# ConvFFN: a fifth buffer for the raw weights, and the partial sums p5 in the place of the constants

## The chip, the core and the metric

The kernel runs on one core of a Trainium2 chip. The metric is the device time of one launch in microseconds, as the median of several runs. A profiled execution has, beside its time, a span: from its first to its last instruction.

## What is computed

One block of a streaming encoder over 512 frames of 1024 channels: two recurrent branches that are merged by gates, a cross-attention into a memory of 256 rows, and a gated ConvFFN. The change lies in the ConvFFN, which is, cut to what matters:

```python
def conv_ffn(h, w_in, conv_w, conv_b, w_out):          # h 512 x 1024, D_FF 2816
    u = h @ w_in                                        # w_in 1024 x 5632
    gate = causal_dwconv(u[..., :D_FF], conv_w, conv_b) # three taps along the frames
    return (jax.nn.gelu(gate) * u[..., D_FF:]) @ w_out  # w_out 2816 x 1024
...
x = x + conv_ffn(rms_norm(x, norm_ffn_g[l]), w_ffn_in[l], ffn_conv_w[l], ffn_conv_b[l], w_ffn_out[l])
return rms_norm(x, norm_final_g)
```

All of it is float32.

## The kernel before

**Weights.** Each weight goes into the products as two numbers of the type fp32r: `hi` is the cast of the raw value and `lo` the raw value minus `hi`. A product is then three matmuls (`mm3`, lines 169 to 173): hi by hi, hi by the low part of the activations, lo by hi. A raw tile of 128 x 1024 numbers (512 KB) comes in by a DMA of the SP queue; ScalarE casts it to `hi`, VectorE subtracts to get `lo`. The pool `wp` has four buffers for raw tiles (tag `wr`) and three each for `hi` (`wh`) and `lo` (`wl`). SP can issue a load when a raw buffer is free, that is when cast and subtraction of the tile that lay in it are done. A cast can run when the matmuls that used its `hi` buffer are done.

**The ConvFFN's two products** are made by a scheme of Strassen's kind with seven products in place of eight: some operands are quarters of the weight matrix (names beginning with A, loaded from the inputs `wfi` and `wfo`), the others (s1, s2, s3, s4) are sums of quarters. These sums are made in HBM by accumulating DMAs of the POOL queue (`w_sums`, line 474, into `dS`; `out_sums`, line 498, into `dO`, named dOs in the profile). `sum_behind` ties each of them to a matmul, which sets their pace. Line 530 copies 704 KB from `dO` to `dO`, four times.

**First product** (lines 1279 to 1334): 22 blocks of 128 channels, two at a time, so 11 groups. Each group makes seven products for both blocks, in the order A11, s1, s2, s4, s3, A12, A22. `stream_quarters` (line 129) brings the weights: one raw tile holds one operand for both blocks, so a group takes seven tiles, 77 in all, and a tile feeds 24 matmuls of 128 x 256. PSUM is emptied on the way: ScalarE copies A11's result to `sn` (line 1287), A11 + s2 to the other half of `sn` (line 1304), and s1's result to `p5` (line 1290); VectorE adds s3's sum to `p5` (line 1309) and at the end of a block multiplies `p5` into the result `graw` (line 1326). `p5` (line 1284; the profile names it p) has a tag of its own with three buffers in the pool `pc`. TensorE goes on accumulating in the same PSUM tile after each copy, so it waits for the copy.

**Second product** (lines 1341 to 1480): the same seven names, four output blocks of eleven units each, with weights from `out_weights` (line 1344): 39 raw tiles, some filled by two DMAs. Between the products the operands are split (`split_g`) on ScalarE and VectorE. The sums of s4 are issued behind the product s2, since they accumulate onto what s2 has read.

**Constants.** `cst` (line 83, pool `cp`) holds an identity, masks and a block of ones, 128 x 896 numbers. Its last use is the identity in the attention's transposes (line 1139), ahead of the ConvFFN.

**Order.** The framework that builds the program orders the instructions of each engine by priority, once, at build time; what is issued under `high_priority` (the loads, casts and subtractions) is put ahead of the rest when it can be. Each engine then works through its list in order, with semaphores where data or a buffer must be waited for.

Of the kernel before, what the change touches and what calls it, by code (L numbers as in the profile page):

```python
# [9 lines left out]
F32 = mybir.dt.float32  # L10
# [7 lines left out]
P = 128  # L18
T = 512
# [35 lines left out]
NCONST = 2 * P + T + P  # L55
# [3 lines left out]
def hybrid_block_kernel(ctx: ExitStack, tc: tile.TileContext, xT_d, mT_d, pv_d, cst_d, win_d, wk_d, wv_d,  # L59
# [4 lines left out]
    wp = ctx.enter_context(tc.tile_pool(name="wp", bufs=3))  # L64
    cp = ctx.enter_context(tc.tile_pool(name="cp", bufs=1))
# [12 lines left out]
    def rw_ps(name, pool=None, tag="rw", **kw):  # L78
        return (pool or prw).tile([P, T], F32, tag=tag, name=name, **kw)


    pv = cp.tile([P, NPV], F32, name="pv")
    cst = cp.tile([P, NCONST], F32, name="cst")
    ident = cst[:, 0:P]
    bones = cst[:, P:2 * P]
    smask = cst[:, 2 * P:2 * P + T]
# [14 lines left out]
    def weight_tiles(name, g, at):  # L101

        hi = wp.tile([P, 1024 + 4 * OFF], F32R, tag="wh", name=f"{name}_h{g}")
        return hi[:, at:at + 1024], wp.tile([P, 1024], F32R, tag="wl", name=f"{name}_l{g}")

    def stream(dram, name, between=None, order=None, at=0):

        for g in order or range(dram.shape[0]):
# [17 lines left out]
                between = None  # L126
            yield hi, lo

    def stream_quarters(srcs, name):

        for g, src in enumerate(srcs):
            with tc.high_priority():
                raw = wp.tile([P, 2, T], F32, tag="wr", name=f"{name}_r{g}", bufs=4)
                wdma.append(nc.sync.dma_start(raw, src))
                hi, lo = (t.rearrange("p (n f) -> p n f", n=2) for t in weight_tiles(name, g, OFF))
                S.copy(hi, raw)  # L136
                V.tensor_tensor(lo, raw, hi.bitcast(F32), ALU.subtract)  # L137
            for i in range(2):
                yield hi[:, i], lo[:, i]

    class Units:
# [10 lines left out]
        def next(self):  # L152
            if self.left == 0:
                self.fill()
            i = self.i
            self.i += 1
            self.left -= 1
            return self.hi[:, i * P:(i + 1) * P], self.lo[:, i * P:(i + 1) * P]

    def sum_exact(ps, blocks, src, pool, tag, name):  # L160

        hi = pool.tile(list(src.shape), F32R, tag=tag, name=f"{name}_h", bufs=2)
        lo = pool.tile(list(src.shape), F32R, tag=tag, name=f"{name}_l", bufs=2)
        S.copy(hi, src)
        V.tensor_tensor(lo, src, hi.bitcast(F32), ALU.subtract)
        PE.matmul(ps, blocks, hi, start=True, stop=False)
        PE.matmul(ps, blocks, lo, start=False, stop=True)
# [1002 lines left out]
    H = T // 2  # L1170
# [53 lines left out]
    pc = ctx.enter_context(tc.tile_pool(name="pc", bufs=2, reuse_waits="tile"))  # L1224
    pf = ctx.enter_context(tc.tile_pool(name="pf", bufs=1, space=PSUM, reuse_waits="tile"))
    rf = pc.tile([P, T], F32, name="rf", bufs=1)
    RHS = {"A11": "B11", "s1": "b1", "s2": "b2", "s4": "B22", "s3": "b3", "A12": "B21", "A22": "b4"}

    def source(m, n):
        if n[0] == "A":  # L1230
            return quarter(m, int(n[1]), int(n[2]), NQ)
        return dS[m // NQ][:, :, SLOT[n], :].rearrange("n p f -> p n f")

    wq = stream_quarters([source(m, n) for m in range(0, FB, NQ) for n in RHS], "wfi")

    def product(n, out, start, nsum=0):
        wh, wl = next(wq)
        b = hop[RHS[n]]
        for i in range(4):
            sl = slice(i * P, (i + 1) * P)  # L1240
            ins = mm3(out, wh[:, sl], wl[:, sl], b[:, 0, i, :], b[:, 1, i, :], start and i == 0, i == 3,
                      skip_group_check=not start)
            if i < nsum:
                sum_behind(ins)
# [34 lines left out]
    for m0 in range(0, FB, NQ):  # L1279
        ms = range(m0, m0 + NQ)  # L1280
        YZ = {m: pf.tile([P, T], F32, tag="yz", name=f"fyz_ps{m}", bufs=4) for m in ms}
        X = {m: pf.tile([P, T], F32, tag="x", name=f"fx_ps{m}", bufs=4)[:, 0:H] for m in ms}
        sn = {m: pc.tile([P, T], F32, tag="sn", name=f"sn{m}", bufs=3) for m in ms}
        p5 = {m: pc.tile([P, H], F32, tag="p5", name=f"p5_{m}", bufs=3) for m in ms}
        for m in ms:
            product("A11", X[m], True, nsum=m - m0)
            S.copy(sn[m][:, 0:H], X[m])
        for m in ms:
            product("s1", YZ[m][:, H:T], True)
            S.copy(p5[m], YZ[m][:, H:T])  # L1290
        if m0 == 0:
            fn_ps = rw_ps("rs_ps", pf, tag="yz", bufs=4)
            sum_exact(fn_ps, onesr, ssf, pc, "ac", "rf")
            sso = cp.tile([P, T], F32, tag="ssq", name="sso")
            with tc.issue_after(ln_exp_set().ins):
                S.activation(rf, fn_ps, AF.Ln, scale=1.0 / D, bias=eps[:, 0:1])
                S.activation(sso, rf, AF.Exp, scale=0.5)
                S.activation(rf, rf, AF.Exp, scale=-0.5)
        elif m0 // NQ <= KB:
            k = m0 // NQ - 1  # L1300
            V.tensor_tensor(xr[:, k, :], xr[:, k, :], sso, ALU.mult)
        for m in ms:
            product("s2", X[m], False, nsum=m - m0)
            S.copy(sn[m][:, H:T], X[m])  # L1304
        for m in ms:
            product("s4", YZ[m][:, H:T], False, nsum=m - m0)
        for m in ms:
            product("s3", X[m], False)
            V.tensor_tensor(p5[m], X[m], p5[m], ALU.add)
        for m in ms:  # L1310
            product("A12", YZ[m][:, 0:H], True, nsum=m - m0)
        for m in ms:
            product("A22", X[m], False, nsum=(m - m0) * (m0 // NQ % 2))
        for m in ms:
            s = pc.tile([P, T], F32, tag="s", name=f"fs{m}")
            V.tensor_tensor(s, YZ[m], sn[m], ALU.add)
            V.tensor_tensor(s, s, rf, ALU.mult)
            ac = pc.tile([P, T], F32, tag="ac", name=f"fa{m}")
            S.activation(ac, s, AF.Identity, scale=par("fcw", 44 + m), bias=par("fcb", m))
            for k in range(1, 3):  # L1320
                V.scalar_tensor_tensor(ac[:, k:], s[:, 0:T - k], par("fcw", 22 * (2 - k) + m), ac[:, k:],
                                       ALU.mult, ALU.add)
            gelu = S.activation(ac, ac, AF.Gelu_apprx_tanh)
            out = graw[:, m]
            V.scalar_tensor_tensor(out[:, 0:H], X[m], -1.0, ac[:, 0:H], ALU.mult, ALU.mult)
            V.scalar_tensor_tensor(out[:, H:T], p5[m], -1.0, ac[:, H:T], ALU.mult, ALU.mult)
            k = m % HB
            if k % 4 == 3 or k == HB - 1:
                k -= k % 4
                if m < HB:  # L1330
                    split_g(0, lambda ks: g1(ks, 1), k)
                    b1_g(k)
                else:
                    b3_g(k)
# [9 lines left out]
    def out_weights():  # L1344

        flat = []
        for n in ("A11", "A12", "s1", "s2", "s3", "A22", "s4"):
            for m, k in out_order:
                if n[0] == "A":
                    p, i = out_units(m, int(n[1]), int(n[2]))[k]  # L1350
                    flat.append((p, wfo_d[p], i))
                else:
                    flat.append(((n, m), dO["s2" if n == "s4" else n, m], k))
        for g in range(0, len(flat), 8):
            units = flat[g:g + 8]
            n = len(units) * P
            with tc.high_priority():
                raw = wp.tile([P, 1024], F32, tag="wr", name=f"wfo_r{g // 8}", bufs=4)
                k = 0
                while k < len(units):  # L1360
                    key, src, i = units[k]
                    e = k
                    while e < len(units) and units[e][0] == key and units[e][2] == i + e - k:
                        e += 1
                    nc.sync.dma_start(raw[:, k * P:e * P], src[:, i * P:(i + e - k) * P])
                    k = e
                hi, lo = weight_tiles("wfo", g // 8, OFF)
                S.copy(hi[:, :n], raw[:, :n])  # L1368
                V.tensor_tensor(lo[:, :n], raw[:, :n], hi[:, :n].bitcast(F32), ALU.subtract)  # L1369
            for k in range(len(units)):  # L1370
                yield hi[:, k * P:(k + 1) * P], lo[:, k * P:(k + 1) * P]
# [27 lines left out]
    p1, p5 = ([t[:, c] for t in ts for c in cols] for ts in (sn1, sn5))  # L1399
# [158 lines left out]
```

## Time and profile before

| | us |
|---|---|
| median of 3 runs | 887.35 |
| lowest and highest of the runs | 886.36, 889.17 |
| the profiled execution | 885.64 |
| its span | 883.9 |
| TensorE (PE) busy | 867.5 |
| VectorE (DVE) busy | 676.8 |
| ScalarE (ACT) busy | 513.3 |
| first matmul of the ConvFFN's first product | 552.9 |

PE is TensorE's matmuls and PEld its weight loads, which overlap them; DVE is VectorE, ACT ScalarE, POOL GpSimd, SP the engine that issues most loads; a q behind an engine's name is its queue of DMA issues. In a table of stretches each row has: the stretch and its length; for PE, PEld, DVE, ACT and POOL the busy time and (x) the count of instructions; TensorE's granted clock; the busy share of the DMA engines; GB/s. In a list of waits a row has who waited, for whom, the total in us, how often, and the longest. In a timeline a row has the start and the length in us, the engine, the line, and in brackets the idle time before it with what ended it.

### The profile page before, as it was taken

The numbers are of one execution on the slowest core, as the hardware profiler recorded it, in microseconds if no ns is written. First come the engines' busy times: TensorE is split into PE (matmuls) and PEld (weight loads), VectorE is DVE, ScalarE is ACT, GpSimd is POOL, SyncE is SP. The second block draws the span as 40 slices with busy tenths as digits, with TensorE's granted clock in tenths as the row PEclk, the third lists the DMA queues.
The fourth block names the chain that finished last, engine by engine and source line by source line (L and its number), as shares of the span: only waits on it lengthen the run. The fifth ranks groups of instructions, "written<-read, shape, count | busy, mean of one in ns | idle before, by whom it ended". The sixth has DMA issues, their size and how long they took to land.

```text
span 883.9 us, 15941 instructions
## 1 busy us (share of the span) xinstructions
PE 867.5 (98%) x6197; PEld 756.8 (86%) x6197; DVE 676.8 (77%) x1096; ACT 513.3 (58%) x788; POOL 132.6 (15%) x163
## 2 busy tenths in 40 slices
PE   8999999999999999999999999999999999999996
PEld 7878878888877677888887778999999999999996
DVE  6796598777976777685575568899888788998674
ACT  6575676643438576334464456766655556767563
POOL 0102223021101022001122211111111211111100
PEclk9999999999999999999999999999999999999998
DMA  7978799678997379758887868999989999998973
GB/s 273 314 250 219 200 228 230 201 186 247 262 238 156 75 191 231 219 170 229 220 237 186 184 146 194 244 262 318 264 247 304 280 293 278 245 284 210 289 214 95
DMA packets 97562, 201.37 MB, mean 228 GB/s; under 512 B 19600, under 2 KB 30992, under 8 KB 97424
## 3 DMA queue, kind: packets, MB, share of 16 engines
q1 hardware_dynamic: 62240, 118.57, 40.7%
q0 software_dynamic: 25504, 67.38, 37.3%
q10 hardware_dynamic: 9744, 14.42, 4.9%
q8 instruction: 48, 0.79, 0.3%
q14 instruction: 26, 0.21, 0.1%
HBM read 188.54 MB, written 78.12 MB: 302 GB/s over the span
## 4 chain that ended last, share of the span: by engine, by line
PE 82%; DVE 7%; DMA 6%; ACT 3%; issue 1%; DVEq 0%; SPq 0%; ACTq 0%
PE in_ps L171 7%; PE in_ps L172 7%; PE in_ps L170 7%; PE fx_ps L170 4%; PE fx_ps L172 4%; PE fx_ps L171 4%; PE fyz_ps L170 3%; PE fyz_ps L172 3%; PE fyz_ps L171 3%; DMA wfi_r<-in_wfi 2%; DMA wfo_r<-dOs 2%; PE q_ps L171 2%; PE co_ps L170 2%; PE mix_ps L171 2%; PE q_ps L172 2%; PE co_ps L172 2%
## 5 line engine op out<-in xcount | busy, mean ns | idle before, releaser
L171 PE MATMUL in_ps<-hT,win_h 128*128 128x512 f32 x304 | 121.1, 398 | 0.4 <-DVE hT L387 0.4
L172 PE MATMUL in_ps<-hT,win_l 128*128 128x512 f32 x304 | 121.3, 399 | 0.0
L170 PE MATMUL in_ps<-hT,win_h 128*128 128x512 f32 x304 | 120.3, 397 | 0.3 <-DVE pr L589 0.3
L136 ACT CAST wfi_h<-wfi_r 128x1024 fp32r<-128x1024 f32 x77 | 80.9, 1051 | 62.8 <-PE fyz_ps L171 13.6
L137 DVE TENSOR_TENSOR wfi_l<-wfi_r,wfi_h 128x1024 fp32r<-128x1024 f32 x77 | 94.0, 1221 | 25.7 <-ACT wfi_h L136 25.3
L485 POOL DMA_DIRECT2D dS<-in_wfi x66 | 66.8, 1028 | 296.2 <-PE in_ps L170 103.7
L171 PEld LDWEIGHTS in_ps<-hT,win_h 128*128 128x128 f32 x304 | 57.1, 188 | 14.6 <-DVE hT L387 1.1
L170 PEld LDWEIGHTS in_ps<-hT,win_h 128*128 128x128 f32 x304 | 57.1, 188 | 13.5 <-DVE pr L589 0.7
L172 PEld LDWEIGHTS in_ps<-hT,win_l 128*128 128x128 f32 x304 | 57.1, 188 | 12.8 <-issue 0.7
L521 POOL DMA_DIRECT2D dOs<-in_wfo x54 | 39.9, 798 | 179.5 <-PE fx_ps L170 55.7
L123 DVE TENSOR_TENSOR win_l<-win_r,win_h 128x1024 fp32r<-128x1024 f32 x38 | 46.3, 1221 | 24.2 <-ACT win_h L122 23.6
L122 ACT CAST win_h<-win_r 128x1024 fp32r<-128x1024 f32 x38 | 39.9, 1049 | 42.4 <-PE in_ps L171 38.0
L1369 DVE TENSOR_TENSOR wfo_l<-wfo_r,wfo_h 128x1024 fp32r<-128x1024 f32 (+1 forms) x39 | 46.9, 1206 | 13.8 <-ACT wfo_h L1368 13.8
L1368 ACT CAST wfo_h<-wfo_r 128x1024 fp32r<-128x1024 f32 (+1 forms) x39 | 40.3, 1035 | 28.5 <-DMA wfo_r<-dOs 11.6
L172 PE MATMUL ox_ps<-go,wfo_l 128*128 128x256 f32 x176 | 49.2, 279 | 1.0 <-DVE wfo_l L1369 1.0
L170 PE MATMUL fyz_ps<-hq,wfi_h 128*128 128x256 f32 x176 | 48.8, 278 | 0.3 <-ACT p L1290 0.3
L170 PE MATMUL fx_ps<-hq,wfi_h 128*128 128x256 f32 x176 | 48.9, 278 | 0.2
L170 PE MATMUL fx_ps<-hr,wfi_h 128*128 128x256 f32 x176 | 48.7, 277 | 0.5 <-ACT sn L1304 0.5
L172 PE MATMUL fyz_ps<-hq,wfi_l 128*128 128x256 f32 x176 | 48.8, 278 | 0.0
L172 PE MATMUL fx_ps<-hq,wfi_l 128*128 128x256 f32 x176 | 48.7, 277 | 0.0
L170 PE MATMUL ox_ps<-go,wfo_h 128*128 128x256 f32 x176 | 48.6, 276 | 0.0
L171 PE MATMUL fyz_ps<-hq,wfi_h 128*128 128x256 f32 x176 | 48.6, 276 | 0.0
(432 smaller groups left out, 2693.7 us busy)
## 6 DMA issues: line engine op xcount, KB each, us to landing
dS<-in_wfi POOLq DMA_DIRECT2D x66, 512.0 KB, 7.6
wfi_r<-dS SPq DMA_DIRECT2D x44, 512.0 KB, 7.0
win_r<-in_win SPq DMA_DIRECT2D x38, 512.0 KB, 5.3
wfi_r<-in_wfi SPq DMA_DIRECT2D x33, 512.0 KB, 5.8
dS<-dS POOLq DMA_DIRECT2D x22, 512.0 KB, 5.6
dOs<-in_wfo POOLq DMA_DIRECT2D x12, 512.0 KB, 8.2
wk_r<-in_wk SPq DMA_DIRECT2D x8, 512.0 KB, 5.1
wv_r<-in_wv SPq DMA_DIRECT2D x8, 512.0 KB, 4.2
```

Source lines behind the costliest of these rows:

```text
L122: casts.append(S.copy(hi[:, o:o + n], raw[:, o:o + n]))
L123: V.tensor_tensor(lo[:, o:o + n], raw[:, o:o + n], hi[:, o:o + n].bitcast(F32), ALU.subtract)
L136: S.copy(hi, raw)
L137: V.tensor_tensor(lo, raw, hi.bitcast(F32), ALU.subtract)
L170: first = PE.matmul(ps, lh, rh, start=start, stop=False, **kw)
L171: PE.matmul(ps, lh, rl, start=False, stop=False, **kw)
L172: PE.matmul(ps, ll, rh, start=False, stop=stop, **kw)
L485: return lambda: nc.gpsimd.dma_start(s(out), src, **kw)
L521: yield lambda k=k, w=w, src=src: nc.gpsimd.dma_start(dO[n, m][:, k * P:(k + w) * P], src, **kw)
L1368: S.copy(hi[:, :n], raw[:, :n])
L1369: V.tensor_tensor(lo[:, :n], raw[:, :n], hi[:, :n].bitcast(F32), ALU.subtract)
```

## The change

The fifth raw buffer lies in the pool `pc`. A counter runs over the raw tiles of both products of the ConvFFN; every fifth tile from the tenth on (10, 15, 20, and so on) takes the buffer in `pc`, all others go round the four in `wp` as before. To make room, `p5` no longer has three buffers in `pc`: it becomes one tile of three slots in the pool `cp` under the tag of `cst`, so that it takes the place of the constants in SBUF, and block m uses slot m modulo 3. `pc` loses 3 KB in each partition and gains 4 KB.

```diff
-    cst = cp.tile([P, NCONST], F32, name="cst")
+    cst = cp.tile([P, NCONST], F32, tag="cst", name="cst")
...
+    nraw = [0]
+
+    def raw_tile(shape, name):
+
+        nraw[0] += 1
+        if nraw[0] > 5 and nraw[0] % 5 == 0:
+            return pc.tile(shape, F32, tag="wr", name=name, bufs=1)
+        return wp.tile(shape, F32, tag="wr", name=name, bufs=4)
...
-                raw = wp.tile([P, 2, T], F32, tag="wr", name=f"{name}_r{g}", bufs=4)
+                raw = raw_tile([P, 2, T], f"{name}_r{g}")
...
+    p5s = cp.tile([P, 3, H], F32, tag="cst", name="p5s")
...
-        p5 = {m: pc.tile([P, H], F32, tag="p5", name=f"p5_{m}", bufs=3) for m in ms}
+        p5 = {m: p5s[:, m % 3] for m in ms}
...
-                raw = wp.tile([P, 1024], F32, tag="wr", name=f"wfo_r{g // 8}", bufs=4)
+                raw = raw_tile([P, 1024], f"wfo_r{g // 8}")
```

## The prediction

> **What bounds the kernel now.** I read the head of the page first, then its chain that ended last.
>
> ```profile
> span 883.9 us, 15941 instructions
> ...
> PE 867.5 (98%) x6197; PEld 756.8 (86%) x6197; DVE 676.8 (77%) x1096; ACT 513.3 (58%) x788; POOL 132.6 (15%) x163
> ...
> PE 82%; DVE 7%; DMA 6%; ACT 3%; issue 1%; DVEq 0%; SPq 0%; ACTq 0%
> ```
>
> TensorE bounds the program: 867.5 of 883.9 us, and 82% of the chain. No edit here changes a matmul, so the change can be worth only the time in which TensorE stands still in the stage that it touches, the ConvFFN (from 553 us to the end). How much is that? The list of waits of TensorE between 520 and 859 us gives three rows:
>
> ```profile
> PE ox_ps L172 <- DVE wfo_l L1369: 1.0, 2, 0.7
> PE fx_ps L170 <- ACT sn L1304: 0.5, 1, 0.5
> PE fyz_ps L170 <- ACT p L1290: 0.3, 1, 0.3
> ```
>
> That is 1.8 us, and it is too little: a matmul of this stage is shown with 276 ns, but they start closer together, so part of each stall lies under the matmul before it. Counting starts is better. In the table of stretches (after the engine's busy us stands the count):
>
> ```profile
> 580.00:590.00 10.00, 9.54 (x83) 9.35 (x83) 8.38 (x13) 5.43 (x8) 0.73 (x2) 1.00 1.00 298
> 600.00:610.00 10.00, 10.00 (x91) 10.00 (x90) 9.04 (x12) 6.25 (x9) 2.76 (x4) 1.00 1.02 284
> ...
> 600.00:680.00 80.00, 80.00 (x708) 80.00 (x707) 70.34 (x94) 51.07 (x77) 13.95 (x20) 1.00 0.95 277
> 700.00:740.00 40.00, 39.39 (x335) 38.47 (x335) 30.81 (x42) 21.34 (x34) 7.10 (x10) 1.00 0.97 274
> 810.00:840.00 30.00, 28.95 (x247) 28.25 (x246) 20.54 (x25) 16.54 (x19) 4.91 (x6) 1.00 1.01 279
> ```
>
> From 600 to 680 us TensorE never stops: 708 matmuls in 80 us, one every 0.113 us (a stretch also counts the two or so that reach into it). At that pace 700 to 740 would hold about 354, and holds 335: 19 x 0.113 = **2.1 us** lost. 810 to 840 would hold 266 and holds 247: **2.1 us**. 580 to 590 holds 83 where 600 to 610 has 91: **0.9 us**. Together **5.1 us**, 0.58% of the run. The granted clock is 1.00 in all five rows, so this is waiting and not throttling.
>
> The Trainium skill (Perfetto Trace Analysis, Identifying the Most-Contended Engine) says that matmul busy time is no measure of TensorE's headroom and that the busy time of the weight loads is. The trace agrees in direction: in the three stretches the matmul column is idle 0.5 + 0.6 + 1.1 = 2.1 us and the weight-load column 0.7 + 1.5 + 1.8 = 3.9 us. By that rule the ceiling would be 3.9 us where the count gives 5.1.
>
> What ends those stalls? The chain in order of time has, in the stage, four long pieces that are no engine's work:
>
> ```profile
> 695.46 8.94 DMA wfi_r<-in_wfi
> ...
> 715.42 9.54 DMA wfi_r<-in_wfi
> ...
> 807.93 9.04 DMA wfo_r<-dOs
> ...
> 819.83 8.40 DMA wfo_r<-dOs
> ```
>
> They are raw weights on their way in, and each stands a few us ahead of the losses just counted. The first stall, at 585, shows how a late load reaches TensorE. ScalarE's timeline:
>
> ```profile
> 583.89 1.05 ACT L136 CAST wfi_h<-wfi_r 128x1024 fp32r<-128x1024 f32 x1 [2.26 <-PE fyz_ps L171]
> 584.85 0.63 ACT L1323 ACTIVATE fa<-fa 128x512 f32<-128x512 f32 x1
> 585.38 0.35 ACT L1304 COPY sn<-fx_ps 128x256 f32<-128x256 f32 x1
> ```
>
> ScalarE works in order. It stood 2.26 us in front of a cast, then did that and a gelu, and only then the copy (L1304) for which TensorE was waiting. The row blames TensorE; that it was a load I infer from its neighbours: the waits of ScalarE from 520 us on name loads as often.
>
> ```profile
> ACT wfi_h L136 <- PE fyz_ps L171: 13.6, 11, 2.3
> ACT wfi_h L136 <- DMA wfi_r<-dS: 11.6, 8, 2.8
> ACT wfo_h L1368 <- DMA wfo_r<-dOs: 11.6, 6, 3.4
> ...
> ACT wfi_h L136 <- DMA wfi_r<-in_wfi: 9.6, 4, 4.6
> ...
> ACT wfo_h L1368 <- DMA wfo_r<-in_wfo: 4.8, 2, 3.0
> ```
>
> The DMA rows make 11.6 + 11.6 + 9.6 + 4.8 = 37.6 us in 20 waits. Now why are the loads late? SP's own waits and the tile of raw weights answer:
>
> ```profile
> SPq L134 <- DVE wfi_l L137: 122.0, 55, 3.4
> SPq L1365 <- DVE wfo_l L1369: 29.1, 16, 2.9
> ...
> L136 ACT CAST wfi_h<-wfi_r x77: 1034/1051/1069, 541.8 to 758.4; 128x1024 fp32r<-128x1024 f32 x77
> L137 DVE TENSOR_TENSOR wfi_l<-wfi_r,wfi_h x77: 1212/1220/1230, 542.9 to 760.5; 128x1024 fp32r<-128x1024 f32 x77
> ...
> DMA to landing us min/median/max: 3.5/6.7/10.8
> ```
>
> In 55 of 77 loads SP waits for the subtraction (L137) that frees a raw buffer. So a load goes out the moment one of four buffers comes free, and no sooner. One buffer therefore goes round in: landing, cast 1.05, subtraction 1.22. A tile feeds 24 matmuls, 24 x 0.113 = 2.7 us, so four buffers allow 10.8 us for the round. With the median landing it takes 6.7 + 2.3 = 9.0 us and fits; with the 8.9 and 9.5 of the chain it takes 11.2 to 11.8, with the worst landing 13.1, and does not.
>
> **The change part by part.** It removes no instruction and adds none: 77 + 39 raw tiles are loaded, cast and subtracted as before.
>
> *The fifth buffer.* From the tenth tile on the round may take 5 x 2.7 = 13.5 us. That is just over the 13.1 us of the worst landing in the trace. So if landings stay as long as they are, all three losses go: 0.9 + 2.1 + 2.1 = 5.1 us, the upper end. But a load issued 2.7 us earlier also means one more in flight. If the engines were so full that each load had to wait for one more, it would cost 0.524 MB (128 x 1024 numbers) at the 277 GB/s of the row of 600 to 680, 1.9 us a round. Then the worst round is 15.0, late by 1.5 us where it is late by 2.3 today, and only (2.3 - 1.5)/2.3 = 35% of 5.1 = 1.8 us is gained, the lower end. Below nothing it goes only by a mechanism among the rivals.
>
> I take **4.0 us**, nearer to the upper end, because the total of bytes is unchanged and the worst landings are not those of a steadily full queue. Around the load of 695.46:
>
> ```profile
> 695.31 0.52 POOL L530 DMA_DIRECT2D dOs<-dOs  x1 [4.63 <-PE fx_ps L170]
> 703.70 1.65 POOL L521 DMA_DIRECT2D dOs<-in_wfo  x2 [7.87 <-DMA dOs<-dOs]
> ...
> DMA  9999209969004000069999997999948986999999
> ...
> 697.26 5.58 SPq L134 DMA_DIRECT2D wfi_r<-dS  x3
> ```
>
> POOL issued a copy inside HBM at 695.31, 0.15 us ahead of the load. The DMA line (695 to 704 us in 40 slices) then shows slices of 0 while both were out. It is one burst that drags this load to 8.94 us where the median is 6.7; a longer round outlasts it. With 2.7 us more lead the load would have been issued at about 692.8, ahead of the copy.
>
> *What else moves.* SP issues nothing but weight loads until the output, so an earlier load pushes no other issue back. Behind the last matmul nothing changes but its start.
>
> *POOL's sums.* They are paced by matmuls and shift with them. More loads in flight can lengthen them, up to the same 1.9 us each. The last is issued at 822.8 us; the loads that read these sums come behind eleven loads of the input that SP issues until 842.4 (831.08 + 11.29), some 20 us later. So nothing; the cover gone, the last product would wait.
>
> ```profile
> L521 POOL DMA_DIRECT2D dOs<-in_wfo x54: 527/813/1437, 590.7 to 822.8; - x54
> ...
> 831.08 11.29 SPq L1365 DMA_DIRECT2D wfo_r<-in_wfo  x11
> ...
> L1139 PE MATMUL prT_ps<-cst,ex x32: 270/273/330, 454.7 to 511.0; 128*128 128x128 f32 x32
> ...
> L1290 ACT COPY p<-fyz_ps x22: 352/372/387, 559.6 to 753.8; 128x256 f32<-128x256 f32 x22
> ...
> L172 PE MATMUL co_ps<-o,wo_l x12: 392/392/398, 545.1 to 552.6; 128*128 128x512 f32 x12
> ```
>
> *p5 in the constants' place.* The last reader of `cst` is the transpose of L1139, which starts at 511.0; the first write of p5 is at 559.6. The new wait has been over for 48 us. Still three slots by m modulo 3, so block m waits for block m - 3 as before: 0 us. If that cover were missing, ScalarE would stand at its first copy, with the casts behind it.
>
> *The first use of the fifth buffer.* Its memory belonged to the attention and the output projection, whose matmuls end with 552.6 + 0.4 us; the tenth load goes out after that (its nine predecessors do). 0 us.
>
> Sum: 885.64 (the profiled execution) - 4.0 = 881.6. That execution is 1.7 us faster than the median of the runs, 887.35; the same 4.0 us from there is **883.3 us**, -0.45%.
>
> **Rivals.**
>
> *The loads land no earlier.* In the stretches with stalls the DMA column stands at 0.97 and 1.01, so the engines may simply be full and the fifth load only queues. The gain is then 1.8 us or less; I price it at 1.0: 886.3. For it: those shares. Against it: 0.95 in the stretch without any stall, so fullness alone does not stall TensorE, and the empty slices above. The Trainium skill (DMA: Bandwidth & Descriptors, Issuing engines are not separate DMA queues) has a rule that speaks for this rival: all queues run on the same 16 engines and interleave. The trace agrees that the POOL copy and the SP load got in each other's way.
>
> *It doesn't do what it says.* The cast also needs one of three hi/lo buffers, which the matmuls free: the 13.6 us row above. Where that wait is the last, a raw tile only lies longer in SBUF. If it is so at the stalls too, the time stays: 887.3. Against it: the four DMA pieces in the chain.
>
> *Slower: the order on ScalarE.* The order of each engine is fixed when the program is built. With raw tiles free sooner, a cast may be put ahead of a copy (L1287, L1290, L1304) that it followed. If its load is then still out, TensorE waits for the copy, as at 585: 0.9 us each. There are 11 groups of two blocks. From five such places on (4.5 us) the gain is gone; in all but three groups it is 8 x 0.9 - 4.0 = +3.2 us: 890.5. Against it: casts are held back by the hi/lo buffers as before, so they have little room to move.
>
> *Slower by far: p5 as one tile.* If the three slots in one tile were held as one, each copy of a group would wait for the last multiply (L1326) of the group before:
>
> ```profile
> 580.99 0.36 ACT L1290 COPY p<-fyz_ps 128x256 f32<-128x256 f32 x1
> ...
> 586.45 0.42 DVE L1326 SCALAR_TENSOR_TENSOR graw<-p,fa 128x256 f32<-128x256 f32 x1
> ```
>
> 5.9 us in each of ten groups, some 55 us. Other tiles here are written and read slice by slice, so I give it little.
>
> **How the numbers follow.** This kernel's measurement tells about 0.3% (2.7 us) from no change. Forecast, a gain of 2.7 to 5.1 us: 0.55. Loads no earlier 0.22 and no effect 0.08, both within 0.3%: 0.30. Order on ScalarE 0.12 and p5 as one tile 0.03: slower 0.15. The range goes from 881.0 (the whole 5.1 from the median is 882.2; the lowest of the runs lies 1.0 under their median) to 888.5 (no effect, plus 1.2 of the runs' spread); it leaves out the two slower cases and little else.
>
> **What would show it.** Right: 700 to 740 us holds about 354 matmuls, 810 to 840 about 266; the chain has no DMA piece of over 8 us behind 560; ScalarE's waits for DMAs fall from 37.6 to under 15 us, those for TensorE rise; SP still waits for L137. The steps are wrong if the waits for loads stay near 37 us (full engines), if the median landing rises from 6.7 to 8.6 or more (the 1.9 us are paid), or if TensorE waits for L1287, L1290 or L1304 at new places (the order).

## The result: 5 to 6 us faster, and where they came from

| | before | changed |
|---|---|---|
| median, first comparison | 887.44 us (6 runs, 886.36 to 889.17) | 881.58 us (6 runs, 880.43 to 882.20) |
| ratio with its 95% interval | | 0.9936 [0.9919, 0.9953] |
| median, compared again on another chip | 886.92 us (19 runs, 882.96 to 892.27) | 881.88 us (8 runs, 880.54 to 885.84) |
| ratio with its 95% interval | | 0.9940 [0.9919, 0.9961] |
| profiled execution, its span | 885.64, 883.9 us | 880.43, 878.6 us |

The gain is 5.9 us in the one comparison and 5.0 us in the other. The prediction said 883.3 us, a gain of 4.0 us from the 887.35 us that it started from. In the profile after, lines of the code behind the edit stand 9 or 10 lower (the cast L136 is now L145, the subtraction L137 is L146, the copy of p5 L1290 is L1300).

The head of the page after, and of its chain the shares by engine:

```profile
span 878.6 us, 15940 instructions
...
PE 864.2 (98%) x6197; PEld 754.2 (86%) x6197; DVE 676.5 (77%) x1096; ACT 514.6 (59%) x788; POOL 132.6 (15%) x163
...
PE 89%; DVE 6%; ACT 2%; DMA 2%; issue 1%; DVEq 0%; ACTq 0%; SPq 0%
```

The chain's share of DMA falls from 6% to 2%, and TensorE's rises from 82% to 89%. Busy time hardly shows it: 867.5 to 864.2 us is 3.3 us of the 5.3 by which the span fell. The stretches show it better. After (the count behind x is what to read):

```profile
550.00:560.00 10.00, 9.65 (x71) 8.85 (x69) 7.96 (x16) 7.09 (x16) 1.14 (x1) 1.00 0.88 197
560.00:570.00 10.00, 10.00 (x85) 9.70 (x84) 7.17 (x11) 6.84 (x10) 1.58 (x3) 1.00 0.97 310
580.00:590.00 10.00, 9.94 (x88) 9.74 (x87) 9.29 (x15) 5.53 (x9) 0.72 (x1) 1.00 0.90 271
600.00:680.00 80.00, 80.00 (x709) 80.00 (x708) 70.32 (x94) 50.76 (x76) 13.95 (x20) 1.00 0.98 282
700.00:740.00 40.00, 40.00 (x355) 40.00 (x355) 33.88 (x46) 23.55 (x35) 7.07 (x10) 1.00 1.00 293
780.00:810.00 30.00, 30.00 (x267) 30.00 (x267) 29.79 (x36) 22.69 (x33) 2.65 (x5) 1.00 0.86 221
810.00:840.00 30.00, 30.00 (x267) 30.00 (x266) 22.43 (x30) 17.37 (x21) 4.78 (x6) 1.00 1.02 295
```

and before, for the three stretches that the prediction did not show:

```profile
550.00:560.00 10.00, 10.00 (x75) 9.30 (x74) 8.03 (x16) 7.05 (x15) 1.14 (x1) 1.00 0.88 190
560.00:570.00 10.00, 10.00 (x86) 9.74 (x85) 8.07 (x12) 7.28 (x11) 1.99 (x3) 1.00 0.94 260
...
780.00:810.00 30.00, 30.00 (x262) 29.68 (x261) 30.00 (x37) 20.69 (x30) 4.12 (x5) 1.00 0.84 245
```

With 0.113 us for a matmul, the ledger of the two profiled executions is: 700 to 740 us 20 matmuls more (2.3 us), 810 to 840 20 more (2.3), 780 to 810 5 more (0.6), 580 to 590 5 more (0.6), 550 to 570 5 fewer (-0.6). The sum is 5.1 us of the span's 5.3. Everything from 600 us on runs at full pace now. Only the start of the stage lost something.

The waits of ScalarE from 520 to 860 us say why:

```profile
ACT wfi_h L145 <- PE fyz_ps L180: 24.7, 20, 1.7
ACT wfi_h L145 <- PE fx_ps L180: 17.2, 16, 1.7
ACT wfo_h L1378 <- DMA wfo_r<-dOs: 10.4, 8, 3.4
```

Of the DMA rows (37.6 us before) one is left, 10.4 us, and no cast of the first product waits for a load any more. The casts now wait for matmuls to free a `hi` buffer: weights lie ready, and TensorE sets the pace. SP still waits for the subtraction:

```profile
SPq L143 <- DVE wfi_l L146: 127.5, 55, 4.2
```

and the loads, by the tile of raw weights, take about as long as before (3.5/6.7/10.8 there):

```profile
DMA to landing us min/median/max: 3.6/6.9/11.3
```

### The profile page after: what moved, and what is told of

It is laid out like the page before. It is cut to its first block, busy times and chain, and to the rows that moved or that the text cites. A ratio compares the mean times of both kernels' runs of the same rounds, so it can differ in the third digit from the quotient of the medians.

```text
span 878.6 us, 15940 instructions
## 1 busy us (share of the span) xinstructions
PE 864.2 (98%) x6197; PEld 754.2 (86%) x6197; DVE 676.5 (77%) x1096; ACT 514.6 (59%) x788; POOL 132.6 (15%) x163
## 4 chain that ended last, share of the span: by engine, by line
PE 89%; DVE 6%; ACT 2%; DMA 2%; issue 1%; DVEq 0%; ACTq 0%; SPq 0%
PE in_ps L180 7%; PE in_ps L179 7%; PE in_ps L181 7%; PE fx_ps L179 4%; PE fx_ps L181 4%; PE fx_ps L180 4%; PE fyz_ps L181 3%; PE fyz_ps L179 3%; PE fyz_ps L180 3%; PE ox_ps L179 2%; PE ox_ps L181 2%; PE ox_ps L180 2%; PE oyz_ps L179 2%; PE oyz_ps L181 2%; PE oyz_ps L180 2%; PE q_ps L180 2%
## 5 line engine op out<-in xcount | busy, mean ns | idle before, releaser
L145 ACT CAST wfi_h<-wfi_r 128x1024 fp32r<-128x1024 f32 x77 | 80.9, 1051 | 69.7 <-PE fyz_ps L180 24.7
L146 DVE TENSOR_TENSOR wfi_l<-wfi_r,wfi_h 128x1024 fp32r<-128x1024 f32 x77 | 94.0, 1220 | 22.5 <-ACT wfi_h L145 22.4
L530 POOL DMA_DIRECT2D dOs<-in_wfo x54 | 39.8, 801 | 168.3 <-PE fx_ps L179 43.2
L1378 ACT CAST wfo_h<-wfo_r 128x1024 fp32r<-128x1024 f32 (+1 forms) x39 | 40.4, 1036 | 24.5 <-DMA wfo_r<-dOs 10.4
L179 PE MATMUL fx_ps<-hq,wfi_h 128*128 128x256 f32 x176 | 48.6, 276 | 0.0
L180 PE MATMUL fx_ps<-hq,wfi_h 128*128 128x256 f32 x176 | 48.6, 276 | 0.0
```

Of the source, the lines that this page charges most:

```text
L179: first = PE.matmul(ps, lh, rh, start=start, stop=False, **kw)
L180: PE.matmul(ps, lh, rl, start=False, stop=False, **kw)
L530: yield lambda k=k, w=w, src=src: nc.gpsimd.dma_start(dO[n, m][:, k * P:(k + w) * P], src, **kw)
```

## The experiments

The theory was: a raw buffer's round (landing, cast, subtraction) did not always fit into four buffers, a fifth makes it fit, and both products gain from that. The rivals: the gain is something that p5's move brought; only single bursts (the copies of L530) made loads late; or the loss at the start of the stage belongs to the load and not to an order of instructions.

### The two halves of the change, and each product by itself

**e1_p5_only** keeps p5 in the constants' place and has four raw buffers:

```diff
-        if nraw[0] > 5 and nraw[0] % 5 == 0:
-            return pc.tile(shape, F32, tag="wr", name=name, bufs=1)
         return wp.tile(shape, F32, tag="wr", name=name, bufs=4)
```

> p5 moved into the constants' place, four raw buffers as before. Theory (the round of the raw buffers is what the change lengthened): nothing is regained, 887.4 us within 1 us, ScalarE waits for loads near the 37.6 us of before, 335 matmuls from 700 to 740 us. Rival (the moved p5, or the places in SBUF and the order that moved with it, made the gain): 882 to 884 us.

**e2_first_only** gives the fifth buffer to the first product alone:

```diff
-                raw = raw_tile([P, 1024], f"wfo_r{g // 8}")
+                raw = wp.tile([P, 1024], F32, tag="wr", name=f"wfo_r{g // 8}", bufs=4)
```

> The fifth buffer for the 77 tiles of the first product alone. Theory: the losses at 580 to 590 (0.9) and 700 to 740 (2.1) go, that of 810 to 840 (2.1) stays: about 884.4 us. The small loss at 780 to 810, where VectorE is full, should stay if it belongs to VectorE alone, and go if VectorE had come late because it had waited for the loads before. Rival (the deeper round only lets the stalls come later): 886 to 887 us.

**e3_second_only** gives it to the second alone, from that product's fifth tile on. The buffer is then free from the start, and the loads of that tile go out early, from 558.8 us, while the first product runs:

```diff
-        if nraw[0] > 5 and nraw[0] % 5 == 0:
+        if nraw[0] % 5 == 0:
...
-                raw = raw_tile([P, 2, T], f"{name}_r{g}")
+                raw = wp.tile([P, 2, T], F32, tag="wr", name=f"{name}_r{g}", bufs=4)
```

> The fifth buffer for the 39 tiles of the second product alone. Theory: only the loss at 810 to 840 us goes (2.1, at most 2.6 with that of 780 to 810): about 885 us; 700 to 740 still holds about 335 matmuls. Together with the run before it the two gains should add up to that of the whole change. Rival (one place carries all): no change here, 887.4 us.

On one chip, with 886.08 us for the kernel before (35 runs, 883.11 to 892.10):

| | median | ratio to before |
|---|---|---|
| p5 alone | 887.58 us | 1.0021 [1.0007, 1.0036] |
| with the fifth buffer in the first product | 883.86 us | 0.9972 [0.9954, 0.9989] |
| with the fifth buffer in the second product | 884.45 us | 0.9978 [0.9960, 0.9995] |

The stretches 700 to 740 and 810 to 840 us of the three, first those of p5 alone:

```profile
700.00:740.00 40.00, 39.48 (x346) 39.29 (x347) 33.45 (x47) 23.89 (x37) 7.07 (x10) 1.00 0.94 280
...
810.00:840.00 30.00, 27.87 (x239) 27.21 (x239) 20.32 (x23) 16.21 (x19) 5.25 (x7) 1.00 1.01 270
```

Then those with the fifth buffer in the first product, and with it in the second:

```profile
700.00:740.00 40.00, 40.00 (x355) 40.00 (x354) 33.26 (x44) 23.89 (x35) 7.07 (x10) 1.00 1.00 293
...
810.00:840.00 30.00, 27.99 (x239) 27.20 (x238) 20.50 (x26) 15.69 (x20) 4.89 (x6) 1.00 1.01 271
```

```profile
700.00:740.00 40.00, 39.85 (x345) 39.28 (x344) 32.46 (x44) 23.44 (x35) 7.13 (x10) 1.00 0.98 283
...
810.00:840.00 30.00, 30.00 (x267) 30.00 (x267) 23.16 (x30) 18.57 (x23) 4.97 (x6) 1.00 1.05 303
```

Four buffers lose in both stretches; the fifth buffer in the first product gives 355 and 239, and in the second product 345 and 267. In these two stretches each product gets back its own stalls and nothing of the other's (e3 still loses 9 matmuls from 780 to 810 us). From p5 alone the first product gained 3.7 us (887.58 - 883.86) and the second 3.1 us (887.58 - 884.45), 6.8 together; less the 1.5 us that p5's move cost, that is 5.3 us, and the whole change gave 5.9 and 5.0. By the intervals in the table each time is known to some 1.3 to 1.6 us either way, so the sums can't be expected to agree more closely. So the gain is the buffer's, and p5's move is a loss.

### Why p5's move costs time

The trace of the changed kernel has an order of instructions that differs from that of before in the first two groups of the first product, from 557 to 586 us, on ScalarE, VectorE and TensorE, and is the same after that. p5 alone has the order of the changed kernel on every engine, so the new order comes with p5 and not with the fifth buffer. ScalarE, before:

```profile
558.02 0.37 ACT L1287 COPY sn<-fx_ps 128x256 f32<-128x256 f32 x1
558.40 1.05 ACT L136 CAST wfi_h<-wfi_r 128x1024 fp32r<-128x1024 f32 x1
559.36 0.36 ACT L1287 COPY sn<-fx_ps 128x256 f32<-128x256 f32 x1
559.62 0.65 ACT L1290 COPY p<-fyz_ps 128x256 f32<-128x256 f32 x2
```

and after, ScalarE and then TensorE:

```profile
557.70 0.36 ACT L1300 COPY p5s<-fyz_ps 128x256 f32<-128x256 f32 x1
557.96 0.37 ACT L1297 COPY sn<-fx_ps 128x256 f32<-128x256 f32 x1
558.23 1.05 ACT L145 CAST wfi_h<-wfi_r 128x1024 fp32r<-128x1024 f32 x1
...
558.34 0.28 PE L180 MATMUL fyz_ps<-hq,wfi_h 128*128 128x256 f32 x1
558.97 0.39 PE L181 MATMUL fyz_ps<-hq,wfi_l 128*128 128x256 f32 x1 [0.35 <-DVE wfi_l L146]
559.19 0.28 PE L179 MATMUL fx_ps<-hq,wfi_h 128*128 128x256 f32 x1
```

With p5 moved, its copy comes ahead of the sn copy. (The move changed two things, the place and the form: one tile of three slots in place of three buffers. Which of them changes the order is not shown.) Behind it TensorE takes the first matmuls of s4 before those of s2 and stands in front of a `lo` half that is being made: 0.63 us from start to start where 0.113 would do. Two more such places follow in the new order (0.27 us at 566.3, 0.34 us at 581.4). Is the order really the price? Two kernels hold the first group's p5 copies behind its two copies of A11's result to `sn`, which gives all five engines the order of before in the ConvFFN:

```diff
-            S.copy(sn[m][:, 0:H], X[m])
+            first = S.copy(sn[m][:, 0:H], X[m])
...
-            S.copy(p5[m], YZ[m][:, H:T])
+            with tc.issue_after(first.ins) if m0 == 0 else nullcontext():
+                S.copy(p5[m], YZ[m][:, H:T])
```

**e5_after_again** is the changed kernel beside them, **e6_pinned** the changed kernel with the hold, **e7_p5_pinned** p5 alone (four raw buffers) with the hold.

> The changed kernel once more, beside the next three on the same chip. If its time is its own and not that of one chip: 880.5 to 882.5 us, narrow, against about 886 to 887 before. If the earlier result was a matter of that chip or of the execution that was profiled: over 883.5 us. In the trace 700 to 740 us holds about 354 matmuls and 810 to 840 about 266.

> The changed kernel, with the p5 copies of the first group held behind the sn copies of that group, which gives each engine the order of instructions of the kernel before. Theory A, that the new order costs TensorE the stalls at 558.3, 566.3 and 581.4 us (0.63 + 0.27 + 0.34 = 1.2 us) and five buffers would have cured those of the old order too: 880.0 to 881.0 us, 0.8 to 1.5 less than the changed kernel on the same chip, and 580 to 590 us holds 90 or 91 matmuls. Theory B, that the old order has stalls at the start of the stage that five buffers don't cure (558, 560 and 585 us, 1.5 us): within 0.5 us of the changed kernel.

> Four raw buffers, p5 in the constants' place, and the p5 copies of the first group held as in the run before, so that the order of instructions is that of the kernel before. Theory A, that the 0.2% that p5's move alone cost (887.58 against 886.08 us) is the new order: within 0.5 us of the kernel before on the same chip. Theory B, that it is the place in SBUF itself or chance: 1.0 to 1.8 us more than the kernel before, as without the hold.

On one chip, before at 886.92 us: the changed kernel 881.88 us; with the hold **880.34 us** (6 runs, 879.08 to 881.06), ratio to before 0.9917 [0.9894, 0.9940]; p5 alone with the hold 885.98 us, ratio 0.9989 [0.9967, 1.0010]. The hold is worth 1.5 us in the changed kernel, and with it p5 alone can't be told from before, where without it it was 0.2% slower. That is theory A of both runs. The first stretches with five buffers and the hold:

```profile
550.00:560.00 10.00, 10.00 (x78) 9.43 (x76) 8.03 (x15) 7.28 (x15) 1.29 (x2) 1.00 0.88 201
560.00:570.00 10.00, 10.00 (x85) 9.73 (x85) 8.08 (x13) 6.95 (x11) 2.43 (x3) 1.00 0.95 328
...
580.00:590.00 10.00, 10.00 (x90) 10.00 (x89) 9.19 (x14) 5.32 (x7) 0.72 (x1) 1.00 0.92 290
```

78 in the first stretch where the changed kernel has 71, and 90 in the last where it has 88: 9 matmuls, 1.0 us. Part of that is the stage's own start, at 552.24 us here and at 552.55 in the changed kernel. Counted from the first matmul of the first product on, the three hundredth after it starts 34.82 us later with the hold and 35.85 in the changed kernel, again 1.0 us. Every trace with the new order takes 35.85 to 36.07 us for it (after, e1, e2, e3, e5). Of those with the old order and four or five buffers, five take 34.80 to 34.83 us (e4, e6, e7, e10, e12), and the three with four buffers that stall near 585 us (before, e9, e11) take 35.46 to 35.74. The hold gives the lowest median of the study; its two ends (879.08 to 881.06) overlap those of the changed kernel (880.54 to 885.84) a little, so the 1.5 us is a difference of medians of 6 and 8 runs, of which the traces account for 1.0.

### Is it the round of the buffers? One buffer fewer

**e4_three_raw** was to keep one of the four buffers from the weights:

```diff
+    held = wp.tile([P, 1024], F32, tag="wr", name="held", bufs=4)
+    V.memset(held[:, 0:1], 0.0)
...
+    V.memset(held[:, 0:1], 0.0)
```

> The kernel before, with one of the four raw buffers held from the start of the ConvFFN to its end, so that three go round. Theory: three tiles last 8.1 us, the round takes 9.0 at the median landing of 6.7; if the landings stay, each of some 112 tiles takes 0.3 us more, +33 us; if they shorten with fewer loads in flight, less, but clearly more than with four: +10 to +33 us, 897 to 920. Rival (the buffers of hi and lo bound the casts, the raw ones do not matter): under +3 us.

It measured 885.87 us, ratio 1.0001 [0.9982, 1.0020], and tells nothing of three buffers. The trace has the two writes side by side:

```profile
L1228 DVE MEMSET held<- x1: 59/59/59, 523.6 to 523.6; 128x1 f32 x1
L1483 DVE MEMSET held<- x1: 59/59/59, 523.7 to 523.7; 128x1 f32 x1
```

The second, which depends on nothing, was ordered up to the first, and the buffer was free again before the stage began. In effect this is the kernel before once more. **e8_three_raw** ties the second write to the last multiply of the first product:

```diff
+            end = V.scalar_tensor_tensor(out[:, H:T], p5[m], -1.0, ac[:, H:T], ALU.mult, ALU.mult)
...
+    with tc.issue_after(end.ins):
+        V.memset(held[:, 0:1], 0.0)
```

> The kernel before with one of the four raw buffers taken by an unused tile that is held until the last multiply of the first product; the second product has four again. Theory A, that a buffer's round (landing, cast 1.05, subtraction 1.22) must fit into its number of buffers times 2.7 us: three allow 8.1 us, the median landing of 6.7 gives 9.0, so up to 0.3 us for each of some 70 tiles: 5 to 21 us more than before, 890 to 908 us, and the gain is reversed over the whole first product, 600 to 680 us holding 640 to 700 matmuls in place of 708; landings shorter than 6.7 us, since one load fewer is in flight, would put it at the lower end. Theory B, that only single late bursts count (copies in HBM that hold one load up): under 3 us more, and 600 to 680 us still holds 705 or more.

It measured 912.95 us (4 runs, 909.88 to 914.38), ratio 1.0281 [1.0250, 1.0313]: 26.0 us more than before. Even the stretch in which the kernel before never stops is slow:

```profile
600.00:680.00 80.00, 74.27 (x636) 73.73 (x636) 61.02 (x81) 44.70 (x66) 11.78 (x17) 0.98 0.85 247
```

The loads land sooner than with four (the tile of raw weights),

```profile
DMA to landing us min/median/max: 3.5/5.9/9.4
```

and yet ScalarE's casts wait for them far longer (its waits from 520 us):

```profile
ACT wfi_h L136 <- DMA wfi_r<-in_wfi: 34.3, 15, 4.4
ACT wfi_h L136 <- DMA wfi_r<-dS: 32.4, 17, 4.5
```

636 matmuls where the kernel before does 708: theory A, against B's "705 or more". Its size was under-called (5 to 21 us). The granted clock is part of it; that is told at the end.

### The copies in HBM, and the spread of the stalls

The prediction held a copy of L530 responsible for the late load of 695.46. **e9_rows_copy** pads each row of the sums by 64 numbers, so that the copy moves 128 rows of 5.6 KB in place of 16 runs of 45 KB, in the kernel before; **e10_pinned_rows** does so with five buffers and the hold; **e11_rows_again** and **e12_before_again** repeat e9 and the kernel before on a further chip, each with another profile.

```diff
-    dO = {(n, m): dr.tile([P, HB * P], F32, name=f"dO{n}_{m}") for n in ("s1", "s2", "s3") for m in range(MQ)}
+    dO = {(n, m): dr.tile([P, HB * P + 64], F32, name=f"dO{n}_{m}") for n in ("s1", "s2", "s3") for m in range(MQ)}
...
-                    yield lambda m=m: nc.gpsimd.dma_start(dO["s2", m], dO["s1", m])
+                    yield lambda m=m: nc.gpsimd.dma_start(dO["s2", m][:, :HB * P], dO["s1", m][:, :HB * P])
```

> The kernel before with four raw buffers; each row of the sums in HBM gets 64 numbers of padding, so that the copies of L530 (4 x 704 KB) go as 128 rows of 5.6 KB in place of 16 runs of 45 KB; the order of instructions stays. Theory A, that such a copy is one burst that drags the load beside it: the longest landings of wfi_r between 660 and 740 us fall from 9 to 11 us to under 8, 690 to 740 us loses nothing, and the time falls by 0.5 to 2 us against the kernel before on the same chip. Theory B, that the loads there are late because four buffers leave no room in a busy stretch whatever the copy's shape: within 0.7 us of the kernel before, 700 to 740 us or its neighbours still lose 1 to 2 us, and the empty DMA slices stay or move.

> Five raw buffers, the p5 copies of the first group held, and the same padded rows in HBM. With five buffers no load ends late there, so both theories expect the time of the version with the hold alone, 880.3 us, within 0.5 us. More than 1 us less would mean that the copies cost something that the matmuls' starts don't show; more than 1 us more would mean that 128 short rows cost the engines more than 16 long runs.

> The padded rows with four raw buffers once more, on another chip and with another profile, because the last time gained 0.2% while its profile (the slowest of its runs) still lost as much between 690 and 840 us as the kernel before. Theory A, the copy as 16 long runs drags the loads: again 1 to 3 us less than before, and this profile loses under 1 us between 680 and 740 us (at most 8 matmuls short of 355 in 700 to 740). Theory B, four buffers are too few in that stretch whatever the shape: again a loss of 1 us or more there, and a time within 1 us of the kernel before on this chip.

> The kernel before itself with another profile, for the spread of its stalls: about 886 to 887 us. If where the stalls fall is chance of the execution: the total lost between 552 and 853 us by the matmuls' starts is again 5 to 7 us, in 810 to 840 us always 2 us or more, while the 0.9 us at 585 and the 2.1 us of 700 to 740 come or go. If they are fixed by the order: the same three places with the same sizes within 0.3 us.

e9: 884.15 us against 886.33, ratio 0.9979 [0.9966, 0.9993]. e11: 884.99 against 886.45, ratio 0.9980 [0.9957, 1.0002]. e10: 880.48 us, the same as the hold without padding. e12: 886.85 us, ratio 1.0004. The profiles of e9 and then e11, from 700 to 740 us:

```profile
700.00:740.00 40.00, 39.26 (x341) 38.77 (x340) 32.80 (x45) 23.04 (x35) 7.13 (x10) 1.00 0.97 274
```

```profile
700.00:740.00 40.00, 40.00 (x355) 40.00 (x355) 32.31 (x43) 23.82 (x35) 7.13 (x10) 1.00 1.00 299
```

One loses 1.6 us there, the other nothing. The kernel before does the same by itself: in e4, which is in effect that kernel, the stretch has 356 matmuls, in e12 337, and in the profile of the prediction 335. The three stretches of the prediction in e12:

```profile
580.00:590.00 10.00, 10.00 (x91) 10.00 (x90) 8.84 (x13) 6.06 (x9) 0.72 (x1) 1.00 0.91 294
700.00:740.00 40.00, 39.16 (x337) 38.51 (x337) 31.79 (x44) 22.71 (x34) 7.11 (x10) 1.00 0.96 278
810.00:840.00 30.00, 27.80 (x238) 27.00 (x237) 20.15 (x25) 16.12 (x19) 4.88 (x6) 1.00 1.00 275
```

So the stall at 585 comes and goes (83 matmuls in the prediction's profile, 91 in e12), that of 700 to 740 comes, goes or moves, and the one in the second product is always there (237 to 247 of 267, 2.3 to 3.4 us). The longest landing is not cured by the padding either (10.8 us before, 11.0 in e9, 10.7 in e11). The medians say that the copies as long runs cost 1.5 to 2.2 us with four buffers, though e11's interval just reaches 1. The traces don't show it: e11 keeps its full pace from 680 to 740 us, as theory A said, but counts 232 matmuls from 810 to 840 us, and over the stage e9 and e11 lose 6.9 and 6.3 us, no less than the kernel before (5.9 to 6.5, counted as in the next section). The traced execution was in both the slowest of its kernel (885.85 and 887.26 us), so this stays open. With five buffers the copies' shape makes no difference (e10).

## Why the prediction was right, and where it was not

**The bound: right.** Stalls of TensorE in the ConvFFN behind late raw weights, counted by starts, 5.1 us. The two stretches in question went to 355 and 267 matmuls, where 354 and 266 were forecast for no stall. One profile overstated how fixed the places are, but not the total: the gaps of over 0.2 us from one start to the next, less 0.113 us each, from the first matmul of the first product to 853 us, sum to 6.0 us in that profile, 6.5 in e12 and 5.9 in e4, to 1.6 and 1.7 us in the two profiles of the changed kernel, and to 1.0 and 1.2 us in the two with the hold. A loss of 5 matmuls from 780 to 810 us was not counted, and it went as well (with four buffers in both products this stretch holds 253 to 267 from profile to profile).

The path was right too. That a late load stood behind the 2.26 us of 583.89 was inferred from neighbours; the trace bears it out. The load of that tile went out at 572.96 and landed at 583.79, after 10.8 us, the longest landing of the 77. At 716.9 us, where 0.62 us pass between two starts, ScalarE's rows name the load themselves:

```profile
716.17 1.05 ACT L136 CAST wfi_h<-wfi_r 128x1024 fp32r<-128x1024 f32 x1 [1.90 <-DMA wfi_r<-dS]
717.12 0.36 ACT L1290 COPY p<-fyz_ps 128x256 f32<-128x256 f32 x1
```

ScalarE stands in front of the cast, and the copy that TensorE needs comes behind it.

**The round of the buffers: right in kind.** ScalarE's waits for loads fell from 37.6 to 10.4 us (under 15 was forecast), those for TensorE rose, and SP still waits for the subtraction. The three-buffer run shows the other side: a round of 5.9 + 2.3 = 8.2 us by the prediction's sum, against 8.1 us allowed, already costs 26 us. The sum is somewhat short: from the start of a cast to the end of its subtraction a median of 2.4 to 2.6 us passes, not 2.3. What a buffer more buys is the time for which a landed tile lies before its cast. For tiles 11 to 75 of the first product its median is 0.1 us with three buffers, 1.1 to 1.6 with four (before, e4, e12) and 3.7 to 4.3 with five (after, e5, e6); within 0.15 us of the landing start 41, 15 to 20, and 1 or 2 of these 65 casts. So the limit is not as sharp as 13.5 us against 13.1 made it look. After the change, the worst landing and the subtraction chain take 11.3 + 2.3 = 13.6 us, over the limit. Its load goes out at 703.93, and its cast starts at 715.33 as soon as the load is in:

```profile
703.93 0.37 SPq L143 DMA_DIRECT2D wfi_r<-in_wfi  x1
...
715.33 1.05 ACT L145 CAST wfi_h<-wfi_r 128x1024 fp32r<-128x1024 f32 x1
```

TensorE did not stop (355 matmuls in that stretch): a single late tile lives on the lead of those before it. With four buffers and their shorter lead the one load behind the stall of 716.9, landed after 9.3 us, was enough.

**The 4.0 us: too small.** This is the term that was mis-sized. It was set between 1.8 us (each load lands 1.9 us later with one more in flight) and 5.1 us (landings stay). The median landings by the number of raw buffers are 5.9 us (three), 6.4 to 6.7 (four: e4, e12, before) and 6.7 to 7.1 (five: e5, after, e6): the fifth cost some 0.3 us of the 1.9 feared. The upper end was the right one: the buffer itself brought 5.1 us by the traces (6.7 us lost with p5 alone, 1.6 in the changed kernel), and 6.8 us by the two halves' medians.

**p5 at 0 us: wrong.** The step asked whether its data would be waited for, and rightly found that wait over for 48 us. It did not ask whether the move changes the order in which the program is built. That cost 1.5 us by the medians (e1 against before, e6 against e5) and 1.0 us by the traces. The rival "the order on ScalarE" named the mechanism, but blamed raw tiles, casts and all groups. It was p5's copies, in the first group: 0.5 us at one place and 0.2 us at each of two. The two errors have opposite signs: by the medians +2.8 us of buffer and -1.5 us of order leave the 1 to 2 us by which the forecast fell short. That it fell short by no more is partly luck.

**The load of 695.46 dragged by a copy: open.** The padded copies gained 0.2%, but a profile with them still shows the stalls and the long landings. In the changed kernel's trace the same copy goes out at 695.28; a load went out 1.8 us ahead of it (693.48) and landed after 4.8 us, as the prediction had it, but the next one, 0.5 us behind the copy (695.77), landed after 7.2 us and not 8.9. So such a copy beside a load does not by itself make the long landing.

**The rivals.** "The loads land no earlier" and "it doesn't do what it says" are ruled out by ScalarE's waits, and p5 as one tile by its copies (L1300), none of which waits for the multiply of a group before (its 5.9 us in ten groups would have made 59 us, not 55). By the rule from the Trainium skill (Perfetto Trace Analysis, Identifying the Most-Contended Engine) the 3.9 us of idle weight loads would have been the ceiling. It was exceeded: in the same three stretches 45 more matmuls start, which is 5.1 us, and the measured gain is 5.0 and 5.9 us. Counting starts at the undisturbed pace was nearer.

## What to carry to other kernels

Where an in-order engine casts streamed tiles, compare the round of a tile's buffer with (number of buffers) x (time a tile feeds); near equality, one buffer more or less decides; here three (in the first product alone), four and five buffers made 913, 887 and 882 us, where the list of TensorE's waits showed 1.8 us to gain. Count lost time by matmul starts against an undisturbed stretch, and take more than one profile before pricing single stalls. And an edit that moves a buffer can reorder instructions where the program is built: compare the order of each engine, and where it worsens, hold the instructions that moved; here that was worth another 1.0 to 1.5 us.

## What the runs showed of the hardware

The granted clock. With three raw buffers TensorE stood still for 2.05 us, until 602.60, and soon after ran at half clock. The end of its wait in the timeline:

```profile
602.60 0.39 PE L170 MATMUL fx_ps<-hq,wfi_h 128*128 128x256 f32 x1 [2.05 <-ACT sn L1289]
```

and stretches of that run in which the clock (the third number from the end) is below 1, with an undisturbed microsecond (from 609) between them:

```profile
605.00:606.00 1.00, 1.00 (x7) 1.00 (x7) 1.00 (x3) 0.76 (x3) 0.00 (x0) 0.50 0.67 190
...
609.00:610.00 1.00, 1.00 (x11) 1.00 (x10) 1.00 (x2) 0.00 (x0) 0.00 (x0) 1.00 0.89 307
...
710.00:715.00 5.00, 5.00 (x32) 5.00 (x32) 4.37 (x6) 3.56 (x7) 0.52 (x1) 0.67 0.92 343
745.00:750.00 5.00, 5.00 (x35) 5.00 (x35) 4.96 (x7) 2.77 (x3) 0.00 (x0) 0.76 0.58 193
...
780.00:810.00 30.00, 26.19 (x214) 25.82 (x214) 24.50 (x32) 17.35 (x22) 5.54 (x8) 0.94 0.86 255
```

In the microsecond from 605 the row counts 7 matmuls where that from 609 counts 11 (both with those that reach in), and the clock column says 0.50. The episodes begin at 604, 710, 744 and 788 us, each 0.3 to 1.5 us after the end of a stall in which 2.2 to 3.5 us passed from one start to the next, and each lasts 3.4 us. In an episode a matmul starts every 0.213 us in place of 0.113, so 16 start where 30 would: 1.6 us each. The four make at most 6.4 of the 26 us, an estimate, since the loads go on landing meanwhile. The Trainium skill (TensorE: Matmul & The Clock Gate, Part 1) says that the clock falls to half after an idle window of about 3.4 us. The trace agrees with the half clock, but not with that length of idle time, and the measurement decides: 2.2 and 2.3 us from start to start, at 741.5 and 600.3, were enough, while 2.2 and 2.8 us, at 578.7 and 653.2, brought no such episode. Stalls of up to 1 us, as in the kernel before, show a clock of 1.00 in every stretch above.
